# The last gate's products over eight steps of the last heads' attention in place of four, and two features' buffers taken in another order

## The chip, the cores and the metric

The kernel runs on one core of a Trainium2 chip. Its engines are TensorE (PE, with PEld for its weight loads), VectorE (DVE), ScalarE (ACT), GpSimd (POOL) and SyncE (SP), each with a queue of its own that it works off in order; data moves by DMA. The metric is the device time of one execution in microseconds (us), as the median of several runs.

## What is computed

A two-layer encoder over 1024 frames and 16 learned meta tokens (T = 1040), 1024 features. Half of a layer's features come from gated linear attention (GLA, 4 heads), half from softmax attention with a forget bias (FoX, 8 heads); both go through one output projection, and a convolutional feed-forward part follows.

```python
for i in range(DEPTH):
    xn = rms_norm(h, attn_norm[i])
    gq, gk, gv, gr, glr, fq, fk, fv, ff = jnp.split(xn @ w_in[i], cuts, axis=-1)
    ...
    o_gla = rms_norm(o_gla, gla_norm[i].reshape(GLA_HEADS, GLA_DV)).reshape(B, L, GLA_WIDTH)
    o_gla = o_gla * jax.nn.silu(gr)
    log_f = jax.nn.log_sigmoid((ff + b_forget[i]).astype(jnp.float32))
    o_fox = forgetting_attention(...)
    o_fox = rms_norm(o_fox, fox_norm[i].reshape(FOX_HEADS, FOX_DH)).reshape(B, L, FOX_WIDTH)
    h = h + jnp.concatenate([o_gla, o_fox], axis=-1) @ w_out[i]
    h = h + conv_ffn(rms_norm(h, ffn_norm[i]), w_up[i], conv_w[i], conv_b[i], w_down[i])
```

## The kernel before

Features lie on partitions, time along the free axis. Every product of two fp32 matrices is made of three matmuls over high and low parts (`mm3`, L253 to L255): high by high, low weight by high, high weight by low. Such a group is called a triple here. An operand is split by `split`: the high half on ACT (L378), the low half on DVE (L379); `xh`/`xl` are the halves of the normed input, `mh`/`ml` those of the attention's output ("mix", eight pairs: features 0 to 3 from GLA, 4 to 7 from FoX). Weights arrive as `raw` and are split by ACT L220 and DVE L222.

**The attention's steps.** `fox` runs 72 steps for a layer and eight more that only finish what is pending. There are four pairs of FoX heads (p = 0 to 3), 18 steps each: five groups of query tiles of 116 rows, two heads, the tiles of the group. Pair p = 3 begins at step 54, so its steps are 54 to 71. At a step PE makes the scores of one query tile (L706, L707, tile `S`); DVE adds the bias and takes the maximum (L714, two instructions for each piece); ACT takes the exponential (L722). Two steps later PE transposes the result (L743, tile `tr`), and ACT and DVE copy the transposes into `PT`, as high and low halves (L378, L379). Three steps behind the last tile of a head's group PE multiplies PT with V (L761, tile `av`), one step later follow the normalisation ("fold", L774 to L789), and two after that the transposed store. For p = 0 to 2 the store writes feature 4 + p to DRAM (`mixd`, L808); for p = 3 it writes feature 7 straight into its mix pair (L381, L382, and L800). GpSimd adds the causal mask to the bias ahead of a score (L879). PSUM holds five banks for `S` and `tr` together, two for `mm` and one for `av`.

**The fill.** Between these pieces PE gets other matmuls, from a list `work`. `plan(p)` makes the list anew when step `starts[p]` comes, after the old one has been drained; the list's rest is spread evenly over the steps that are left until the next start:

```python
starts = [f + 4 for f in first] + [first[3] + 8, len(steps) + 8]
...
fill_us = work.left / max(starts[p_next] - n, 1)
```

With `first` = 0, 18, 36, 54 the starts are 4, 22, 40, 58, 62 and 80. `plan(3)`, at step 58, is the gate of GLA head 3: `gr_products` multiplies the normed input with the gate's weights, three chunks of 348, 348 and 344 columns, the 344 last, eight features in each (24 triples), and each chunk is turned into feature 3 by six DVE operations (L666, L669, L673, L674, L675, L677) and three of ACT (L670 to L672), which write into the buffer `land[3]`. For the other heads the result goes to `mixd` (L679). Features 4, 5, 0, 1, 2 are loaded from `mixd` at the same time (L994).

`plan(4)`, at step 62, begins the output projection: it loads feature 6 (three pieces, L999), splits the seven features (`one`) chunk by chunk (columns 256, then 384, then 400), loads the residual `h` over each buffer once it is split (L1015, on POOL's queue), and multiplies for the first four of eight output tiles, three chunks each, seven features in the order `KORD` = 4, 5, 0, 1, 2, 3, 6; DVE adds the residual (L1020). Feature 7 and the other output tiles follow after the steps (tile `wo`).

**The buffers.** `slots` hands out 33 SBUF buffers of [128, T] from a list, first in, first out; a new user waits for the last readers of the old one. `land` are the seven buffers `h` of the unsplit features, `mix` the eight pairs. At `plan(4)` the pairs of the normed input (`nm["x"]`) and the norm's factor `r` go back to the list.

Names with numbers (`ml_6126`) are buffers in the tables of instructions below. They are not the same in the two kernels.

## Time and profile before

| | us |
|---|---|
| median of 3 runs | 2537.56 |
| lowest and highest run | 2532.59, 2539.26 |
| profiled execution, its own time | 2536.43 |
| its span in the trace | 2534.6 |
| granted TensorE clock over the span | 0.995 |

The span runs from the first to the last instruction of the profiled execution; the 1.8 us between span and time lie around it. Busy times are sums of an engine's instructions; a window's row gives them for one stretch, with the number of instructions in brackets. In a timeline's row, the first number is the start from the span's beginning, the second the length; matmuls overlap, so that the step from start to start is what one costs. A row's bracket gives the idle time of the engine ahead of it and what ended it. The changed stretch lies at about 437 to 505 us in layer 0 and 1690 to 1755 us in layer 1.

### The profile page before, as it was taken

The numbers are of one execution on the slowest core, as the hardware profiler recorded it, in microseconds if no ns is written. First come the engines' busy times: TensorE is split into PE (matmuls) and PEld (weight loads), VectorE is DVE, ScalarE is ACT, GpSimd is POOL, SyncE is SP. The second block draws the span as 40 slices with busy tenths as digits, with TensorE's granted clock in tenths as the row PEclk, the third lists the DMA queues.
The fourth block names the chain that finished last, engine by engine and source line by source line (L and its number), as shares of the span: only waits on it lengthen the run. The fifth ranks groups of instructions, "written<-read, shape, count | busy, mean of one in ns | idle before, by whom it ended". The sixth has DMA issues, their size and how long they took to land.

```text
span 2534.6 us, 48445 instructions
## 1 busy us (share of the span) xinstructions
PE 2475.4 (98%) x19266; PEld 2417.2 (95%) x19266; DVE 1741.0 (69%) x3373; ACT 1281.9 (51%) x2592; POOL 406.2 (16%) x582
## 2 busy tenths in 40 slices
PE   8999999999999999999999999999999999999998
PEld 7989999899999999999999899999999999999997
DVE  7656676859877777853565666677697777787545
ACT  7346666646444445641353566665464444455312
POOL 4033333210000000100211334331100000001002
PEclk9999999999999999999999999999999999999999
DMA  3132134342322224864312222143432222257622
GB/s 122 65 94 68 45 94 127 118 135 76 118 76 80 81 80 131 202 161 115 105 54 69 74 80 73 62 146 105 141 92 92 80 84 76 80 168 177 190 64 77
DMA packets 116211, 258.25 MB, mean 102 GB/s; under 512 B 14624, under 2 KB 31296, under 8 KB 115984
## 3 DMA queue, kind: packets, MB, share of 16 engines
q1 hardware_dynamic: 92832, 181.74, 23.0%
q0 software_dynamic: 22432, 72.68, 10.4%
q8 instruction: 151, 2.47, 0.4%
q10 hardware_dynamic: 720, 0.74, 0.1%
q14 instruction: 76, 0.62, 0.1%
HBM read 174.50 MB, written 67.81 MB: 96 GB/s over the span
## 4 chain that ended last, share of the span: by engine, by line
PE 83%; DVE 8%; ACT 3%; DMA 2%; issue 2%; POOL 1%; SPq 0%; DVEq 0%; POOLq 0%; ACTq 0%
PE up L253 11%; PE up L254 11%; PE up L255 11%; PE mm L253 8%; PE mm L255 7%; PE mm L254 7%; PE down L253 5%; PE down L254 5%; PE down L255 5%; PE av L761 3%; PE tr L743 2%; PE wo L253 1%; PE wo L255 1%; PE wo L254 1%; DVE P L714 1%
## 5 line engine op out<-in xcount | busy, mean ns | idle before, releaser
L253 PE MATMUL up<-x,hi 128*128 128x260 f32 (+1 forms) x2464 | 697.2, 283 | 2.2 <-DVE hg L1287 1.4
L255 PE MATMUL up<-x,hi 128*128 128x260 f32 (+1 forms) x2464 | 695.9, 282 | 2.4 <-DVE x L1109 2.4
L254 PE MATMUL up<-x,lo 128*128 128x260 f32 (+1 forms) x2464 | 696.6, 283 | 0.0
L255 PEld LDWEIGHTS up<-x,hi 128*128 128x128 f32 x2464 | 465.7, 189 | 3.2 <-DVE x L1109 3.2
L253 PEld LDWEIGHTS up<-x,hi 128*128 128x128 f32 x2464 | 464.5, 189 | 3.1 <-DVE hg L1287 1.8
L254 PEld LDWEIGHTS up<-x,lo 128*128 128x128 f32 x2464 | 464.6, 189 | 0.1
L1085 DVE TENSOR_TENSOR lo<-raw,hi 128x512 fp32r<-128x512 f32 x364 | 249.0, 689 | 178.2 <-ACT hi L1084 170.4
L253 PE MATMUL mm<-xh,hi 128*128 128x348 f32 (+4 forms) x1056 | 363.5, 344 | 0.0
L254 PE MATMUL mm<-xh,lo 128*128 128x348 f32 (+4 forms) x1056 | 339.7, 322 | 0.0
L255 PE MATMUL mm<-xl,hi 128*128 128x348 f32 (+4 forms) x1056 | 339.6, 322 | 0.0
L1084 ACT CAST hi<-raw 128x512 fp32r<-128x512 f32 x364 | 224.6, 621 | 144.2 <-PE up L255 84.8
L253 PEld LDWEIGHTS mm<-xh,hi 128*128 128x128 f32 x1056 | 200.2, 190 | 5.8 <-issue 4.6
L254 PEld LDWEIGHTS mm<-xh,lo 128*128 128x128 f32 x1056 | 200.0, 189 | 0.6 <-issue 0.3
L255 PEld LDWEIGHTS mm<-xl,hi 128*128 128x128 f32 x1056 | 198.9, 188 | 0.6 <-issue 0.3
L254 PE MATMUL down<-ah,lo 128*128 128x260 f32 (+1 forms) x704 | 198.3, 282 | 0.2 <-DVE lo L222 0.2
L255 PE MATMUL down<-al,hi 128*128 128x260 f32 (+1 forms) x704 | 198.2, 282 | 0.0
L253 PE MATMUL down<-ah,hi 128*128 128x260 f32 (+1 forms) x704 | 198.0, 281 | 0.0
L379 DVE TENSOR_TENSOR PT<-tr,PT 116x464 fp32r<-116x464 f32 (+3 forms) x240 | 122.7, 517 | 71.9 <-ACT PT L378 69.7
L220 ACT CAST hi<-raw 128x512 fp32r<-128x512 f32 (+1 forms) x160 | 97.1, 609 | 148.0 <-PE down L255 116.5
L743 PE MATMUL tr<-ident,P 116*116 116x116 f32 x704 | 144.8, 269 | 3.0 <-DVE m L714 2.5
L722 ACT ACTIVATE P<-P,m 116x924 f32<-116x924 f32 (+4 forms) x144 | 110.6, 768 | 70.8 <-DVE m L714 65.2
L1312 POOL DMA_DIRECT2D actd<-cv x44 | 23.6, 537 | 766.1 <-DVE cv L1311 745.1
(300 smaller groups left out, 5782.0 us busy)
## 6 DMA issues: line engine op xcount, KB each, us to landing
raw<-in_wm_dram SPq DMA_DIRECT2D x322, 256.0 KB, 2.8
raw<-in_wd_dram SPq DMA_DIRECT2D x64, 256.0 KB, 3.7
actd<-cv POOLq DMA_DIRECT2D x22, 520.0 KB, 3.0
actd<-cv POOLq DMA_DIRECT2D x22, 512.0 KB, 3.1
cb<-cd SPq DMA_DIRECT2D x16, 520.0 KB, 4.3
st<-actd SPq DMA_DIRECT2D x14, 520.0 KB, 5.4
st<-actd SPq DMA_DIRECT2D x14, 512.0 KB, 5.7
kA<-kA SPq DMA_DIRECT2D x24, 260.0 KB, 4.3
```

Source lines behind the costliest of these rows:

```text
L220: nc.scalar.copy(hi[:, :n, :], raw[:, :n, :])
L253: nc.tensor.matmul(ps, wh, xh[:, c0:c0 + n], start=first, stop=False, skip_group_check=more)
L254: nc.tensor.matmul(ps, wl, xh[:, c0:c0 + n], start=False, stop=False, skip_group_check=more)
L255: nc.tensor.matmul(ps, wh, xl[:, c0:c0 + n], start=False, stop=last, skip_group_check=more)
L379: nc.vector.tensor_tensor(out=lo, in0=src, in1=hi.bitcast(F32), op=ALU.subtract)
L714: nc.vector.tensor_tensor_reduce(out=x, in0=S[:rows, :n], in1=cb[:rows, c0:k1], scale=1.0, scalar=(BIG if ci == 0 else m[:rows, ci - 1:ci] ...
L722: nc.scalar.activation(x, x, AF.Exp, scale=-1.0, bias=low, accum_out=(den if nch < 3 else d2[:rows, 0:1]))
L743: nc.tensor.transpose(tr[:w, j, :rows], P[:rows, o:o + w], id_)
L761: nc.tensor.matmul(av[:, a:width], w.rearrange("p a b -> p (a b)"), x, start=(t == 0 and i == 0), stop=(t == last and i == 1))
L1084: nc.scalar.copy(hi[:, :nk, :], src[:, :nk, :])
L1085: nc.vector.tensor_tensor(out=lo[:, :nk, :], in0=src[:, :nk, :], in1=hi[:, :nk, :].bitcast(F32), op=ALU.subtract)
L1312: nc.gpsimd.dma_start(self.actd[j][:, o0:T], uo)
```

## The change

The start of `plan(4)` moves from step 62 to step 66, so that the gate's 72 matmuls of `plan(3)` spread over steps 58 to 65. What `plan(4)` issues moves with it. `plan(3)` now takes six `h` buffers and the eighth mix pair (`seven`), which the last store needs ahead of step 66. `plan(4)` first gives back the normed input's buffers, then takes the buffer of feature 6, loads into it, and takes seven mix pairs.

```diff
-        starts = [f + 4 for f in first] + [first[3] + 8, len(steps) + 8]
+        starts = [f + 4 for f in first] + [first[3] + 12, len(steps) + 8]
...
                     elif p == 3:
-                        land = box["land"] = [s.get(F32, f"h{k}") for k in range(KD - 1)]
+                        land = box["land"] = [s.get(F32, f"h{k}") for k in range(KD - 2)]
+                        box["seven"] = s.get(F32R, "mh7"), s.get(F32R, "ml7")
                         for k in (4, 5, 0, 1, 2):
                             nc.gpsimd.dma_start(land[k][:, :T], self.mixd[k][:])
                         self.gr_products(lyr, 3, w, ap, pp, nm, land[3])
                     elif p == 4:
-                        land = box["land"]
-                        for c0, n in reversed(CH):
-                            nc.gpsimd.dma_start(land[6][:, c0:c0 + n], self.mixd[6][:, c0:c0 + n])
                         for x in nm["x"]:
                             s.put(*x)
                         s.put(nm["r"])
-                        mix = box["mix"] = [(s.get(F32R, f"mh{k}"), s.get(F32R, f"ml{k}")) for k in range(KD)]
+                        land = box["land"] + [s.get(F32, "h6")]
+                        for c0, n in reversed(CH):
+                            nc.gpsimd.dma_start(land[6][:, c0:c0 + n], self.mixd[6][:, c0:c0 + n])
+                        mix = [(s.get(F32R, f"mh{k}"), s.get(F32R, f"ml{k}")) for k in range(KD - 1)] + [box["seven"]]
+                        box["mix"] = mix
...
-                self.fox(lyr, ap, pp, qs, plan, lambda: box["mix"][KD - 1])
+                self.fox(lyr, ap, pp, qs, plan, lambda: box["seven"])
```

On PE the projection's first triple before stands right behind the scores of step 62 (460 and 116 columns, the transposes of step 60 between them):

```order
L706 MATMUL S<-kA_4642,qA_4640 116x460
L707 MATMUL S<-kL_4644,qA_4640 116x460
L743 MATMUL tr<-ident,P 116x116
L706 MATMUL S<-kA_4642,qA_4640 116x116
L743 MATMUL tr<-ident,P 116x116
L707 MATMUL S<-kL_4644,qA_4640 116x116
L743 MATMUL tr<-ident,P 116x116
L253 MATMUL mm<-mh_6121,hi 128x256
L254 MATMUL mm<-mh_6121,lo 128x256
L255 MATMUL mm<-ml_6122,hi 128x256
```

In the changed kernel it stands behind the scores of step 66 (344 columns), and the last gate triples (`xh`, `xl`) come ahead of them, behind step 65:

```order
L253 MATMUL mm<-xh_147,hi 128x344
L254 MATMUL mm<-xh_147,lo 128x344
L255 MATMUL mm<-xl_148,hi 128x344
L774 MATMUL fo<-ident,avs 116x128 x4
L761 MATMUL av<-PT_6158,V_4646 128x232 x8
L743 MATMUL tr<-ident,P 116x116
L706 MATMUL S<-kA_4642,qA_4640 116x344
L707 MATMUL S<-kL_4644,qA_4640 116x344
L743 MATMUL tr<-ident,P 116x116 x3
L253 MATMUL mm<-mh_6272,hi 128x256
L254 MATMUL mm<-mh_6272,lo 128x256
L255 MATMUL mm<-ml_6273,hi 128x256
```

The gate's products have moved by up to four steps, and the projection's by four. On DVE the low halves before stand in steps 60 to 63; this is the place of step 62, from its score on (`h_5795` is feature 6, `h_5792` feature 3, which L677 finishes here):

```order
L714 ISA P,m<-S,cb 116x460
L714 ISA m 116x1
L677 SCALAR_TENSOR_TENSOR h_5792<-gy,gog 128x344
L714 ISA P,m<-S,cb,m 116x116
L714 ISA m 116x1
L379 TENSOR_TENSOR PT_6152<-tr,PT_6152 116x4x116
L379 TENSOR_TENSOR ml_6126<-h_5795,mh_6125 128x256
L379 TENSOR_TENSOR ml_6122<-h_5793,mh_6121 128x384
L379 TENSOR_TENSOR ml_6124<-h_5794,mh_6123 128x384
L379 TENSOR_TENSOR ml_6116<-h_5790,mh_6115 128x384
L379 TENSOR_TENSOR ml_6118<-h_5791,mh_6117 128x384
```

In the changed kernel the low halves begin in step 63. This is DVE from the score of step 65 on, where the last gate chunk (L666 to L673) and the fold (L778) stand among them; `h_6260` is feature 6:

```order
L714 ISA P,m<-S,cb 116x460
L714 ISA m 116x1
L379 TENSOR_TENSOR ml_6273<-h_5793,mh_6272 128x256
L379 TENSOR_TENSOR PT_6158<-tr,PT_6158 116x4x116
L666 TENSOR_TENSOR gx<-mm,r 128x344
L379 TENSOR_TENSOR ml_6275<-h_5794,mh_6274 128x256
L669 TENSOR_SCALAR ge<-gx 128x344
L673 TENSOR_TENSOR gog<-gx,gog 128x344
L778 TENSOR_TENSOR ff<-fo,ff 116x256
L222 TENSOR_TENSOR lo<-raw,hi 128x512
L379 TENSOR_TENSOR ml_6277<-h_6260,mh_6276 128x256
```

The last low half that the projection's first chunk needs (feature 6) has moved from the score of step 62 to that of step 65 on DVE, while its product has moved from step 62 to step 66 on PE. The low halves' number, and that of every other instruction on PE, DVE and ACT, is the same in both.

## The prediction

> **What bounds the kernel now.** I read the page's head and busy line first, then TensorE's waits, then the stretch around the edit in tables by window and in time order.

> ```profile
> span 2534.6 us, 48445 instructions
> PE 2475.4 (98%) x19266; PEld 2417.2 (95%) x19266; DVE 1741.0 (69%) x3373; ACT 1281.9 (51%) x2592; POOL 406.2 (16%) x582
> ```

> TensorE (PE) is busy for 98% of the span, so nothing can be gained except where PE waits or runs at a lower clock. The edit adds and removes no instruction on PE, DVE or ACT, so its worth lies in those waits. The next rows are a wait table (total, times, longest), first for the whole trace, then for the stretch 418 to 480 us of layer 0, and PE's timeline at the three long waits (start, length, instruction, in brackets the idle time before it).

> ```profile
> PE mm L255 <- DVE ml L379: 7.2, 4, 3.0
> ...
> PE S L706 <- DVE m L714: 0.8, 1, 0.8
> ...
> PE tr L743 <- DVE m L714: 0.3, 1, 0.3
> PE S L706 <- DVE PT L379: 0.2, 1, 0.2
> ```

> ```profile
> 466.19 0.39 PE L255 MATMUL mm<-ml,hi 128*128 128x256 f32 x1 [0.65 <-DVE ml L379]
> ...
> 470.19 0.50 PE L255 MATMUL mm<-ml,hi 128*128 128x256 f32 x1 [2.97 <-DVE ml L379]
> ...
> 1720.98 0.58 PE L255 MATMUL mm<-ml,hi 128*128 128x256 f32 x1 [2.96 <-DVE ml L379]
> ```

> The reader is to see one place per layer: the output projection's first chunk waits 0.65 and then 2.97 us for the low half of features that DVE splits; both layers together lose 7.2 us. The tables by window (length, then busy time of PE, PEld, DVE, ACT, POOL, the granted clock, DMA) say why and what follows.

> ```profile
> 457.00:480.00 23.00, 19.37 (x130) 18.26 (x129) 22.88 (x66) 16.98 (x44) 8.38 (x16) 0.93 0.46 139
> 470.20:473.70 3.50, 3.50 (x13) 3.26 (x14) 3.50 (x9) 2.48 (x8) 1.38 (x3) 0.51 0.16 33
> 1720.90:1726.50 5.60, 5.52 (x20) 5.19 (x21) 5.25 (x14) 3.74 (x11) 2.08 (x4) 0.51 0.27 72
> ```

> From 457 to 480 us DVE is busy for 22.88 of 23.00 us: there **DVE is the bound**, and PE waits for it. Right after the wait the granted clock is 0.51 for 3.5 us in layer 0 and for 5.6 us in layer 1, which costs 3.5 x 0.49 = 1.7 and 5.6 x 0.49 = 2.7 us. Three smaller waits at step 59 of layer 0 (0.8, 0.3, 0.2, by their rows in time 0.77, 0.25, 0.21) add 1.2; layer 1 has none there. All that the edit could save is so 7.2 + 1.7 + 2.7 + 1.2 = **12.8 us**, 0.5% of the span.

> **The change part by part.** Durations are taken from start to start in rows that follow one another without a wait.

> ```profile
> 459.68 0.32 PE L253 MATMUL mm<-xh,hi 128*128 128x344 f32 x1
> ...
> 460.15 0.32 PE L253 MATMUL mm<-xh,hi 128*128 128x344 f32 x1
> ...
> 461.81 0.44 PE L706 MATMUL S<-kA,qA 128*116 128x460 f32 x1
> ...
> 462.68 0.36 PE L253 MATMUL mm<-mh,hi 128*128 128x256 f32 x1
> ...
> 466.41 0.28 PE L253 MATMUL mm<-mh,hi 128*128 128x256 f32 x1
> 466.53 0.28 PE L254 MATMUL mm<-mh,lo 128*128 128x256 f32 x1
> ...
> 474.62 0.33 PE L255 MATMUL mm<-ml,hi 128*128 128x384 f32 x1
> ...
> 475.15 0.34 PE L255 MATMUL mm<-ml,hi 128*128 128x384 f32 x1
> 475.32 1.05 PE L761 MATMUL av<-PT,V 112*128 112x232 f32 x8
> 476.21 0.26 PE L743 MATMUL tr<-ident,P 116*116 116x116 f32 x1
> ```

> So a gate triple takes 0.47 us, a matmul of the projection 0.12 (256 columns) or 0.53 / 3 = 0.18 (384), a step's scores with their transposes 0.87, a block of eight av products 0.89.

> ```profile
> 458.37 0.63 DVE L714 CUSTOM_DVE_ANT_0 P<-S,cb 116x460 f32<-116x460 f32 x1
> 458.92 0.08 DVE L714 DVE_READ_ACCUMULATOR2_ANT m<- 116x1 f32 x1
> ...
> 460.20 0.64 DVE L379 TENSOR_TENSOR PT<-tr,PT 116x464 fp32r<-116x464 f32 x1
> 460.75 0.52 DVE L675 SCALAR_TENSOR_TENSOR gy<-ge,gy 128x348 f32<-128x348 f32 x1
> 461.19 0.42 DVE L379 TENSOR_TENSOR ml<-h,mh 128x256 fp32r<-128x256 f32 x1
> 461.53 0.51 DVE L677 SCALAR_TENSOR_TENSOR h<-gy,gog 128x348 f32<-128x348 f32 x1
> ...
> 464.43 1.29 DVE L222 TENSOR_TENSOR lo<-raw,hi 128x512 fp32r<-128x512 f32 x2
> ...
> 469.71 2.29 DVE L379 TENSOR_TENSOR ml<-h,mh 128x256 fp32r<-128x256 f32 x5
> ...
> 475.44 3.48 DVE L379 TENSOR_TENSOR ml<-h,mh 128x400 fp32r<-128x400 f32 x7
> 478.83 0.63 DVE L714 CUSTOM_DVE_ANT_0 P<-S,cb 116x460 f32<-116x460 f32 x1
> ```

> On DVE a score takes 0.55 + 0.09, a copy of four transposes (PT) 0.55, a low half 0.34 at 256 columns, 3.39 / 7 = 0.48 at 400 and about (2.21 - 0.34) / 4 = 0.47 at 384, a gate operation 0.43 (the clamp of L669 0.25, taken from its neighbours), a weight split 0.6.

> *The start of the projection, from step 62 to 66.* The 72 gate matmuls (24 triples, 11.3 us) are spread over eight steps, and the projection's products begin four steps later. With order and durations, PE's steps 63 to 67 now hold 27 gate matmuls (4.3), 21 + 21 of the projection (2.5 + 3.7), 6 steps' score products (2.0), 31 transposes (2.8) and 32 av products (3.6): **18.9 us**. DVE's same steps hold all 21 low halves (7 x 0.33 + 7 x 0.47 + 7 x 0.48 = 8.9), two gate chunks (2 x 2.4), nine PT copies (3.4), six scores (3.1), two weight splits (1.2), the last head's halves and fold (2.0) and two residual adds (0.8): **24.2 us**. The long wait goes, but the DVE work that caused it is not moved with PE's: some 7 us of PE's filler leave steps 58 to 68 for the steps after the last head, where DVE is idle, and in steps 63 to 67 DVE is short of time by 24.2 - 18.9 = 5.3 us. What is late next is not the projection's operand but the attention itself.

> I follow it from PE's score of step 63 (t = 0), DVE's loads from score to score being 5.5, 4.7, 5.3, 4.5 and 4.2 us. DVE takes up score 63 at 0.75 and, with some 0.75 of small waits on ACT as an estimate, score 64 at 7.0. PE's steps 63 and 64 take 3.7 + 3.2 with small gaps, so that it wants a bank for score 65 at 6.9; it gets one when DVE has copied the transposes of step 64, behind score, low half, small score and copy: 7.0 + 0.64 + 0.34 + 0.28 + 0.55 = 8.8. **PE waits 2.0.** DVE's score 65 comes at 7.0 + 4.7 = 11.7 and the next PT copy is done at 11.7 + 0.64 + 0.34 + 0.55 = 13.2; PE's score, transposes, nine gate matmuls and fold have then taken 2.6 since 8.9, so the av products wait 13.2 - 11.5 = **1.7**. The scores 66, 67 and 68 come to DVE at 17.0, 21.5 and 25.7; PE reaches the av products of step 68 at 22.4 and their PT is done 1.9 behind score 67, at 23.4: **1.0**. Sum 4.7 us per layer, of the 5.3 that the loads gave; the buffers hold the rest.

> *Step 59.* With the fill of steps 58 to 61 halved, PE comes to the score of step 59 three triples earlier, 1.41 us. DVE is held there by the store of an earlier gate chunk, which the edit does not touch.

> ```profile
> 441.68 0.34 DVE L669 TENSOR_SCALAR ge<-gx 128x348 f32<-128x348 f32 x1 [1.91 <-DMA mixd<-ge]
> ...
> 1692.53 0.34 DVE L669 TENSOR_SCALAR ge<-gx 128x348 f32<-128x348 f32 x1 [0.25 <-DMA mixd<-ge]
> ```

> One gate operation (0.44) moves behind DVE's second score of step 58, so layer 0 waits 1.2 + 1.4 - 0.4 = **2.2 us**; in layer 1, whose hold is 0.25 and whose slack I estimate at 0.3, 1.4 - 0.4 - 0.3 = **0.7**.

> *The buffers.* Feature 6 is now loaded into the buffer of xh0, behind PE's last reading of it, which stands ahead of the score of step 64, while its first product follows step 66: more than 7 us for loads that land in 2.7 (from issue to landing, 200 KB).

> ```profile
> h<-mixd POOLq DMA_DIRECT2D x2, 200.0 KB, 2.7
> ```

> They stand on POOL's queue behind the mask of step 64 and ahead of the residual loads and of the mask for step 65, whose score DVE takes at 11.7; with xh0 read by about 3 they have over 8 us. I cost them at nothing; without that cover each microsecond is one of PE's wait. The last pair's buffers are taken before the store that fills them, at nothing.

> *Sum.* After: 2 x 4.7 + 2.2 + 0.7 = 12.3, and the clock stays up if no wait reaches the 2.97 that preceded the fall. Before: 12.8. The difference is -0.5 us, on the profiled execution's 2536.43 gives 2535.9, which lies 1.7 below the median of the runs (2537.56). **I forecast 2536.0 us.** The unshown price is what a wait of about 2 us does to the clock: nothing, or in each layer a window like those above. The bounds are so 0 and 2 x 2.7 = 5.4 us; I take 0, by the nearest row (the wait of 0.65 at 466.19 is followed by products of 0.12 us, full speed).

> [...]

> **The rivals.** *First, the waits of after are hidden.* DVE's shortage needs the order and rates as I have them; if banks come free earlier (ACT shares the PT copies, four steps' lead) and PE is never held in steps 63 to 68, after has no more than step 59's 2.9 us at worst and about 0.4 at best. The gain is 12.8 - 2.9 to 12.8 - 0.4, say 11: 2525.5 us. For it speaks that DVE starts step 63 with little behind it (a load of 1.9 us in step 62 against PE's 3.4); against it the sum of loads, 5.3 us that five banks cannot hold.

> *Second, on the other side: the clock falls all the same.* The waits of 2.0 and 1.7 lie within some 6 us, and PE's halved filler leaves no reserve. If together they bring the clock to 0.51 for as long as in layer 1 (5.6 us), each layer loses 2.7 more; some of it is absorbed, as PE would have waited 1.0 behind. That is +3.4 to +5.4: 2539.3 to 2541.3. If at the same time DVE's lag is 7 rather than 4.7 per layer, 4.6 more: about 2546, slower than the bound below. It decides from the point where the two waits together pass the 3.6 us of before: mine give 3.7 in two pieces.

> *Third, the change does not do what it says:* the long wait stays, as feature 6 comes late in the new buffer. Then 12.8 stays and step 59's 1.7 is added: 2538. The over 7 us of cover speak against it.

> **How the numbers follow.** About 0.3% (7.6 us) is what a measurement of this kernel can tell from no change. Chances: my sum, with an error of some 4 us either way, 0.62; the first rival 0.16; the second 0.16, half of it beyond 0.3%; the third 0.06. Faster by over 0.3%, below 2530: the first rival with 0.02 of the sum's lower edge, 0.18. Slower, above 2545: 0.08. The rest is 0.74. The range goes from 2528.5 to 2543.5: it leaves out most of the first rival and the worst of the second.

> **What would show it.** In the wait table of after, the 7.2 us on the projection's low halves are gone, and in their place stand waits of PE's score and av products for DVE's PT and scores, 4 to 5 us per layer, none over 2.5; step 59's wait in layer 0 is about 2 us; the clock between steps 63 and 68 stays near 1.0; and DVE's busy share there is near 100%. I am wrong if PE shows under 3 us of waits per layer there (first rival), or a window at half clock (second).

## The result, and the profile after

The changed kernel takes 2549.05 us (median of 5 runs, 2544.11 to 2551.03), the kernel before 2534.35 in the same comparison (5 runs, 2532.12 to 2539.26). The ratio is **1.0044, with a 95% interval from 1.0033 to 1.0056**: slower by some 11 us, 8 to 14 by the interval (the two medians alone lie 14.7 us apart). The forecast was 2536.0. The profiled execution took 2549.36 us.

First the page's head and busy line of the changed kernel:

```profile
span 2547.6 us, 48454 instructions
PE 2480.7 (97%) x19266; PEld 2420.5 (95%) x19266; DVE 1742.6 (68%) x3373; ACT 1281.4 (50%) x2592; POOL 407.0 (16%) x582
```

PE, PEld, DVE, ACT and POOL have as many instructions as before (the head's total is 9 higher; the busy line does not show them), and nearly the same busy times: what was added is waiting. These are TensorE's waits in the stretch of layer 0 (420 to 533 us; total, times, longest):

```profile
PE av L761 <- DVE PT L379: 3.1, 4, 1.2
PE tr L743 <- DVE m L714: 2.0, 1, 2.0
PE S L706 <- DVE m L714: 1.5, 2, 1.0
PE av L761 <- ACT PT L378: 1.2, 1, 1.2
...
PE fo L774 <- ACT avs L764: 0.5, 1, 0.5
```

The wait for the projection's low halves (7.2 us in both layers) is gone. In its place layer 0 has 8.3 us of waits of the attention's own matmuls, layer 1 7.8 by the same view; before, the same stretches had 5.5 and 3.9 us, the projection's included. (A wait of 0.8 us at the first `wo` matmul, which both kernels have in both layers, is left out of these sums.) In time order, TensorE's waits of layer 0 (bracket: idle time and what ended it):

```profile
429.27 0.32 PE L761 MATMUL av<-PT,V 112*128 112x112 f32 x1 [1.24 <-DVE PT L379]
...
446.12 0.31 PE L743 MATMUL tr<-ident,P 116*116 116x116 f32 x1 [2.02 <-DVE m L714]
446.85 0.47 PE L706 MATMUL S<-kA,qA 128*116 128x460 f32 x1 [0.42 <-DVE m L714]
...
468.50 1.05 PE L761 MATMUL av<-PT,V 112*128 112x232 f32 x7 [1.15 <-DVE PT L379]
...
473.84 0.47 PE L706 MATMUL S<-kA,qA 128*116 128x460 f32 x1 [1.05 <-DVE m L714]
...
476.82 0.54 PE L774 MATMUL fo<-ident,avs 128*116 128x128 f32 x3 [0.47 <-ACT avs L764]
...
478.56 0.38 PE L761 MATMUL av<-PT,V 112*128 112x232 f32 x1 [1.20 <-ACT PT L378]
479.29 1.84 PE L761 MATMUL av<-PT,V 112*128 112x232 f32 x7 [0.36 <-DVE PT L379]
```

The rows lie at step 55 (429), step 59 (446), the end of step 63 (468), the scores of step 65 (473.84) and the end of step 65 (476 to 479). The tables by window (length, busy time of PE, PEld, DVE, ACT, POOL, granted clock, DMA) show steps 65 to 67 of both layers, and three windows in which the clock fell:

```profile
473.84:492.04 18.20, 16.17 (x95) 15.20 (x95) 18.17 (x52) 13.42 (x38) 7.18 (x13) 0.81 0.55 168
1731.55:1748.36 16.81, 14.79 (x94) 13.86 (x95) 16.81 (x49) 13.42 (x38) 6.10 (x11) 0.90 0.54 165
...
448.20:451.40 3.20, 3.20 (x14) 2.99 (x13) 2.98 (x9) 1.66 (x5) 0.55 (x1) 0.50 0.33 111
478.90:485.70 6.80, 6.44 (x31) 6.34 (x30) 6.80 (x19) 6.80 (x21) 1.08 (x2) 0.50 0.59 218
1738.30:1741.70 3.40, 3.40 (x19) 3.40 (x17) 3.40 (x11) 3.40 (x10) 0.23 (x1) 0.51 0.76 282
```

DVE is busy for 18.17 of 18.20 and 16.81 of 16.81 us in steps 65 to 67, and the clock is at half for 13.4 us in all, against 9.1 us before (waits at its start left out); taken at half of that, the loss is 6.7 us against 4.4. This is an estimate, and a little high: in the changed kernel a matmul of 256 columns took 0.21 us from start to start at half clock and 0.12 elsewhere (medians of 23 and 1984).

The account: waits in the two stretches went from 9.4 to 16.1 us (+6.7), the clock costs 2.3 more, together +9.0. From the first score of step 54 to the first `wo` matmul TensorE took 106.40 us in layer 0 and 105.26 in layer 1 before, and 112.31 and 109.22 after: **+5.9 and +4.0, so +9.9 us**. The 0.9 left stands in no wait and in no half-clock window. Over the runs below, what is left in this way grows with the number of waits, by some 0.27 us for each (an estimate, from a straight line through both layers of the 17 traces with the same matmuls; e4 against e5 has 21 waits against 9, and 3.0 us are left); by this estimate a wait costs a little more than its length. The two profiled executions differ by 12.9; the other 3.0 lie in small parts in other stretches and were not followed.

The table gives the time from one step's first score to the next one's, from those rows of each trace (layer 0 / layer 1, us); e4, e5, e9 and e13 are experiments below.

| steps | before | after | e5 (62, store moved) | e4 (66, store moved) | e9 (e4, no low halves) | e13 (e9, late high halves) |
|---|---|---|---|---|---|---|
| 58 | 7.1 / 5.7 | 7.1 / 6.1 | 5.7 / 5.7 | 4.8 / 4.6 | 4.8 / 4.5 | 4.8 / 4.5 |
| 59 to 61 | 17.0 / 16.7 | 14.2 / 14.2 | 16.9 / 16.9 | 14.3 / 14.0 | 14.0 / 14.5 | 14.0 / 14.2 |
| 62, 63 | 14.4 / 15.4 | 8.4 / 8.4 | 14.4 / 15.1 | 8.2 / 8.4 | 8.4 / 8.2 | 8.4 / 8.4 |
| 64 | 3.9 / 3.8 | 4.4 / 4.4 | 3.9 / 3.8 | 4.4 / 4.4 | 4.0 / 4.0 | 3.7 / 3.7 |
| 65 to 67 | 12.3 / 12.2 | 18.2 / 16.8 | 12.3 / 12.2 | 16.9 / 16.4 | 18.6 / 18.4 | 14.3 / 14.3 |
| 54 to `wo` | 106.4 / 105.3 | 112.3 / 109.2 | 104.9 / 105.2 | 108.2 / 106.5 | 108.7 / 108.7 | 104.6 / 104.0 |

The long stall of steps 62 and 63 is gone, and steps 65 to 67 take 4 to 6 us more. The filler that left comes back behind them: steps 68 to 70 take 2.0 us more in either layer, the last step and its tail up to the `wo` matmul 5.3.

### The profile page after: what moved, and what is told of

The parts are those of the page before. It is cut to its first block, busy times and chain, and to the rows that moved or that the text cites. A ratio compares the mean times of both kernels' runs of the same rounds, so it can differ in the third digit from the quotient of the medians.

```text
span 2547.6 us, 48454 instructions
## 1 busy us (share of the span) xinstructions
PE 2480.7 (97%) x19266; PEld 2420.5 (95%) x19266; DVE 1742.6 (68%) x3373; ACT 1281.4 (50%) x2592; POOL 407.0 (16%) x582
## 4 chain that ended last, share of the span: by engine, by line
PE 50%; issue 31%; DVE 11%; DMA 4%; ACT 3%; POOL 2%; SPq 0%; DVEq 0%; POOLq 0%; ACTq 0%
PE mm L253 8%; PE mm L255 7%; PE mm L254 7%; PE down L253 5%; PE down L255 5%; PE down L254 5%; PE av L761 3%; PE tr L743 2%; DVE P L714 1%; PE wo L253 1%; PE wo L255 1%; PE wo L254 1%; DVE lo L1087 1%; DMA mixd<-ge 1%; PE S L706 1%
## 5 line engine op out<-in xcount | busy, mean ns | idle before, releaser
L253 PE MATMUL up<-x,hi 128*128 128x260 f32 (+1 forms) x2464 | 697.1, 283 | 2.4 <-DVE hg L1289 1.4
L255 PE MATMUL up<-x,hi 128*128 128x260 f32 (+1 forms) x2464 | 696.4, 283 | 2.3 <-DVE x L1111 2.3
L254 PE MATMUL up<-x,lo 128*128 128x260 f32 (+1 forms) x2464 | 696.7, 283 | 0.0
L255 PEld LDWEIGHTS up<-x,hi 128*128 128x128 f32 x2464 | 465.2, 189 | 3.1 <-DVE x L1111 3.1
L253 PEld LDWEIGHTS up<-x,hi 128*128 128x128 f32 x2464 | 464.5, 188 | 3.5 <-DVE hg L1289 1.8
L254 PEld LDWEIGHTS up<-x,lo 128*128 128x128 f32 x2464 | 464.8, 189 | 0.1
L253 PE MATMUL mm<-xh,hi 128*128 128x348 f32 (+4 forms) x1056 | 366.1, 347 | 0.0
L255 PE MATMUL mm<-xl,hi 128*128 128x348 f32 (+4 forms) x1056 | 341.4, 323 | 0.0
L254 PE MATMUL mm<-xh,lo 128*128 128x348 f32 (+4 forms) x1056 | 341.1, 323 | 0.0
L253 PEld LDWEIGHTS mm<-xh,hi 128*128 128x128 f32 x1056 | 201.2, 191 | 5.9 <-issue 4.6
L254 PEld LDWEIGHTS mm<-xh,lo 128*128 128x128 f32 x1056 | 201.2, 191 | 0.6 <-issue 0.3
L255 PEld LDWEIGHTS mm<-xl,hi 128*128 128x128 f32 x1056 | 200.3, 190 | 0.6 <-issue 0.3
L254 PE MATMUL down<-ah,lo 128*128 128x260 f32 (+1 forms) x704 | 198.2, 282 | 1.4 <-DVE lo L222 1.4
L255 PE MATMUL down<-al,hi 128*128 128x260 f32 (+1 forms) x704 | 198.5, 282 | 0.0
L253 PE MATMUL down<-ah,hi 128*128 128x260 f32 (+1 forms) x704 | 198.2, 281 | 0.0
L379 DVE TENSOR_TENSOR PT<-tr,PT 116x464 fp32r<-116x464 f32 (+3 forms) x240 | 122.5, 516 | 70.8 <-ACT PT L378 68.5
L743 PE MATMUL tr<-ident,P 116*116 116x116 f32 x704 | 144.6, 269 | 5.8 <-DVE m L714 5.3
L1069 DVE TENSOR_TENSOR raw<-raw,raw 128x512 f32<-128x512 f32 x198 | 129.8, 688 | 25.3 <-DMA raw<-in_wd_dram 19.1
```

Of the source, the lines that this page charges most:

```text
L253: nc.tensor.matmul(ps, wh, xh[:, c0:c0 + n], start=first, stop=False, skip_group_check=more)
L254: nc.tensor.matmul(ps, wl, xh[:, c0:c0 + n], start=False, stop=False, skip_group_check=more)
L255: nc.tensor.matmul(ps, wh, xl[:, c0:c0 + n], start=False, stop=last, skip_group_check=more)
L379: nc.vector.tensor_tensor(out=lo, in0=src, in1=hi.bitcast(F32), op=ALU.subtract)
L743: nc.tensor.transpose(tr[:w, j, :rows], P[:rows, o:o + w], id_)
L1069: nc.vector.tensor_tensor(out=q[out][:, :nk, :], in0=q[a][:, :nk, :], in1=q[b][:, :nk, :], op=op)
```

## The experiments

Each was compared with the kernel before on the same chip; ratios are to it, with the 95% interval. One thousandth is 2.5 us.

**e1: the order of buffers alone.**

```diff
-        starts = [f + 4 for f in first] + [first[3] + 12, len(steps) + 8]
+        starts = [f + 4 for f in first] + [first[3] + 8, len(steps) + 8]
```

> The start of the projection back at step 62, the changed order of buffers kept. Theory A (VectorE's low halves and gate work hold up the attention in steps 62 to 67, and TensorE's waits there and at step 59 bring the clock down, all because the filler moved): the time is near that of before, 2532 to 2540 us, with the long wait for a low half back. Rival B (feature 6 in the buffer of xh0 comes late and delays the rest): 2545 us or more, with waits of ScalarE for the load of feature 6.

Measured: 2540.18 us, 1.0014 [1.0005, 1.0022]. The buffers alone cost some 3.5 us, 1.3 to 5.6. No wait for the load of feature 6 shows on TensorE or on ScalarE; TensorE's waits for low halves are 2.8 and 3.3 us per layer, and waits for PT of 1.2 us stand beside them. Rival B, 10 us, falls; but the buffers are not free, as both the forecast and theory A had it.

**e2: the start half way**, `first[3] + 10`.

> The projection starts at step 64, half way. Theory A: between the two, 2535 to 2545 us, the waits for PT and scores smaller than the 4.5 us per layer of the changed kernel in these steps, the wait for low halves under 1 us. Rival (only the clock windows matter, not the waits): the time jumps to either end, by whether a window at half clock is there.

Measured: 2543.15 us, 1.0035 [1.0022, 1.0048], in the range of theory A. Rival "only the clock windows matter", which had the time jump to either end, falls. But the waits did not shrink as expected: for low halves none is left, and for PT and scores steps 62 to 67 have 5.2 us in layer 0 and 4.8 in layer 1, where less than 4.5 was forecast.

**e3: the later low halves kept back on VectorE.** `self.scored` is the latest score instruction on VectorE; `issue_after` puts what is written in it behind that instruction on the same engine.

```diff
                             def one(k):
-                                self.split(mix[k][0][:, c0:c0 + n], mix[k][1][:, c0:c0 + n], land[k][:, c0:c0 + n])
+                                if j == 2:
+                                    self.split(mix[k][0][:, c0:c0 + n], mix[k][1][:, c0:c0 + n], land[k][:, c0:c0 + n])
+                                    return
+                                with tc.issue_after(self.scored.ins):
+                                    self.split(mix[k][0][:, c0:c0 + n], mix[k][1][:, c0:c0 + n], land[k][:, c0:c0 + n])
```

> The changed kernel with the low halves of the second and third chunk (384 and 400 columns) kept behind the score of the step in which their unit is written, so that VectorE makes them later, behind the attention's work. Theory A: the waits of steps 62 to 67 fall from 4.5 to under 2 us per layer and the half-clock windows behind them (6.8 us long in layer 0, 3.4 in layer 1) go; 8 to 11 us less than the changed kernel, about 2538 to 2541 us. Rival C (the gate's evacuation or ScalarE holds the attention, not the low halves): no more than 3 us less, 2546 to 2549 us.

Measured: 2549.65 us, 1.0057 [1.0046, 1.0069]: nothing gained. A window of its trace shows where the wait went:

```profile
469.00:477.00 8.00, 5.61 (x30) 4.73 (x28) 6.32 (x16) 8.00 (x24) 2.16 (x4) 0.77 0.43 150
```

DVE is now busy for 6.32 of 8.00 us, but ACT for all of them. The edit held back the low halves only; ACT went on making high halves early, and TensorE waited for ACT's `avs` and `PT`. Of the two forecasts rival C, no gain, was met; theory A as I had it, VectorE alone, fell here.

**e4: the store taken from another tile.** In the kernels shown, the gate's result of heads 0 to 2 stands in the tile `ge`, of which there is one, until it is stored; the next chunk waits for that.

```diff
-            to = e if dst is None else dst[:, c0:c0 + n]
+            to = og if dst is None else dst[:, c0:c0 + n]
...
-                nc.gpsimd.dma_start(self.mixd[h][:, c0:c0 + n], e)
+                nc.gpsimd.dma_start(self.mixd[h][:, c0:c0 + n], og)
```

> The changed kernel, with the gate's result for heads 0 to 2 written into and stored from the tile of the output gate (two buffers) in place of the exponent's tile (one buffer), so that the next gate chunk no longer waits for the store. Theory A: the waits at step 59 (2.0 + 0.4 us and a half-clock window of 3.4 us in layer 0, 1.1 + 0.4 in layer 1) go: about 5 us less, 2544 us. Rival (TensorE comes to step 59 early and waits for VectorE in any case): no change, 2549 us.

Measured: 2537.11 us, 1.0008 [0.9999, 1.0016], some 9 us less than the changed kernel by the ratios; I had expected 5. Step 58 falls from 7.1 and 6.1 to 4.8 and 4.6 us. VectorE's row in the changed kernel's timeline shows the hold that went, 2.58 us against 1.91 before:

```profile
444.78 0.34 DVE L669 TENSOR_SCALAR ge<-gx 128x348 f32<-128x348 f32 x1 [2.58 <-DMA mixd<-ge]
```

The same trace holds the best view of the clock. These are TensorE's waits at the end of step 65 in layer 0 and in layer 1, and the windows behind them:

```profile
470.18 0.54 PE L774 MATMUL fo<-ident,avs 128*116 128x128 f32 x3 [0.47 <-ACT avs L764]
471.92 0.37 PE L761 MATMUL av<-PT,V 112*128 112x232 f32 x1 [1.20 <-ACT PT L378]
472.65 1.38 PE L761 MATMUL av<-PT,V 112*128 112x232 f32 x7 [0.36 <-DVE PT L379]
...
1724.28 0.54 PE L774 MATMUL fo<-ident,avs 128*116 128x128 f32 x3 [0.48 <-ACT avs L764]
1726.02 0.37 PE L761 MATMUL av<-PT,V 112*128 112x232 f32 x1 [1.20 <-ACT PT L378]
1726.75 1.05 PE L761 MATMUL av<-PT,V 112*128 112x232 f32 x7 [0.36 <-DVE PT L379]
```

```profile
473.20:476.70 3.50, 3.50 (x19) 3.43 (x18) 3.50 (x11) 3.50 (x11) 0.00 (x0) 0.51 0.78 290
1727.20:1730.70 3.50, 3.50 (x33) 3.48 (x32) 3.50 (x11) 3.50 (x10) 0.00 (x0) 1.00 0.82 286
```

Behind the same three waits, 2.0 us within 3, the clock was 0.51 in layer 0 and 1.00 in layer 1.

**e5: the same edit on the kernel before.**

> The kernel before, with only the store of the gate's result taken from the tile of the output gate (as in e4). It is the base against which e4 is read. If the store's hold costs only what shows at step 59 of layer 0: 1 to 2 us less than before, 2533 to 2535 us. If e4's gain of 12 us came from everywhere: 2526 us or less, and the start at step 66 would then still cost some 11 us over this.

Measured: 2529.77 us, 0.9981 [0.9972, 0.9990]: 5 us faster than before, more than I had put down to step 59, and faster than both kernels. Against this base e4 is slower by 2.7 thousandths, 7 us: **that is what the later start costs without the store's hold, buffers included** (some 4 to 10 us by the two intervals; the last row of the table shows 4.5 of it). In that stretch TensorE's waits are 4.1 us longer in e4 and the rest, which grows with their number, 3.0, while the clock costs 2.5 less (1.7 against 4.2): without the hold it is not the clock that makes the later start slower.

**e6: e4 with the later halves kept back on both engines**, behind `self.exped[-2]`, the exponential of the step before the last, on ScalarE; the low halves need the high ones and follow.

> e4 (start at step 66, store from the output gate's tile), with the high halves on ScalarE of the second and third chunk, and so the low halves that follow them, kept behind the exponentials of the step before the last. Theory D (halves made too early on both engines stand ahead of the copies that the attention waits for): the waits for PT and avs in steps 62 to 66, 5 to 6 us per layer in e4, fall to under 3, and no half-clock window follows: 2530 to 2533 us. Rival E (the chain from score to PT is too long for steps of 3.4 to 5 us, whatever else the engines do): no change, 2536 to 2539 us.

Measured: 2537.05 us, 1.0007 [0.9998, 1.0016], as e4. No window at half clock is left, yet steps 65 to 67 of layer 0 are no shorter:

```profile
466.13:483.61 17.48, 14.37 (x94) 12.06 (x95) 16.69 (x48) 14.99 (x43) 5.67 (x11) 1.00 0.39 125
```

DVE is busy for 16.69 of 17.48 us, and waits for low halves (1.6 us) and PT (3.5) stand where those for ACT stood. By the time rival E was met and theory D was not; but with VectorE this full, the load and the order could not yet be told apart.

**e7: e4 with more matmuls in steps 63 to 65.** The 24 matmuls of the last gate chunk are issued twice (`if twice: self.mm3(...)` ahead of the real one), so that the gate's argument is doubled in these 344 columns.

> e4, with each triple of the last gate chunk (steps 63 to 65) multiplied twice into the same sum, so that this gate is that of a doubled argument in 344 columns: 24 more matmuls of 0.16 us per layer, 7.5 us of TensorE time in all, with nothing added on the other engines. If TensorE only waits in these steps for the others (theory D and rival E alike), the matmuls fill waits and keep the clock up: 2534 to 2540 us. If the waits are not what costs the time there: 2544 us or more.

Measured: 2539.72 us, 1.0019 [1.0011, 1.0028], 2.8 us above e4 for 7.5 us of work, in the range for "fills waits": some 4.7 of it, by the difference and with its noise of some 3 us, stood in time that TensorE would have lost anyway.

**e8: e5 with a gate product on GpSimd**, `nc.gpsimd.tensor_tensor` in place of `nc.vector.tensor_tensor` for L673.

> e5, with the product of the gate's argument and the output gate (L673) on GpSimd in place of VectorE, in all gate chunks. Of the kernel before, theory A says that VectorE is the bound at steps 60 to 62 and that the 3 us wait shrinks by what is taken off it, three operations of 0.43 us: about 1.3 us per layer, and the half-clock window may go with it: 2528 to 2532 us. Rival: GpSimd takes longer and the gate is later: 2535 us or more.

Measured: 2545.73 us, 1.0041 [1.0027, 1.0055], 15 us slower than e5; the rival held. The operation took 984 ns there on average (24 of them), by the groups of its trace:

```profile
L673 POOL TENSOR_TENSOR gog<-gx,gog 128x348 f32<-128x348 f32 (+1 forms) x24 | 23.6, 984 | 21.6 <-DVE gx L666 20.4 <-DVE fv L785 1.2
```

The wait for low halves fell to 2.1 us per layer, as hoped, but waits for scores and PT came in its place all over the attention.

**e9 and e10: the low halves left out.** TensorE multiplies the high half in their place; the seven features' low parts are missing from the projection. e9 has the start at step 66, e10 at step 62.

```diff
-                                self.split(mix[k][0][:, c0:c0 + n], mix[k][1][:, c0:c0 + n], land[k][:, c0:c0 + n])
+                                nc.scalar.copy(mix[k][0][:, c0:c0 + n], land[k][:, c0:c0 + n])
```

> e4 (start at step 66), with the low halves of the seven features left out: TensorE multiplies the high half once more in their place, as many matmuls as before, and VectorE has 21 operations (8.9 us) less per layer in these steps. Theory A (VectorE is the bound in steps 65 to 67, where it was busy for 100% of 16.4 to 18.2 us): TensorE's waits in steps 62 to 67 fall from 5 to 6 us to about 2 per layer, steps 65 to 67 from 16.9 and 16.4 us to 13 to 14: 2529 to 2532 us. Rival E (the latency of the chain from score to PT, or ScalarE): steps 65 to 67 stay above 15.5 us, 2535 us or more.

> e5 (start at step 62) without the same low halves. Theory A: the 3 us wait at step 62 and its half-clock window go, 5 to 6 us per layer: 2518 to 2521 us, and e9 stands above it by what the chain's latency alone costs at the later start. If VectorE is the only reason against the later start, e9 and e10 agree within 3 us; if the thinner filler costs by itself (rival E), e9 is 6 us or more above e10.

Measured: e9 2537.64 us, 1.0005 [0.9994, 1.0017]; e10 2531.99 us, 0.9988 [0.9978, 0.9998]. Both forecasts were missed: with 8.9 us of VectorE's work per layer gone, neither is faster than with it beyond the intervals (e4 1.0008, e5 0.9981). Rows of e9, layer 0: steps 65 to 67 by window, two of TensorE's waits, and ScalarE's queue at that time.

```profile
466.70:485.26 18.56, 16.17 (x95) 15.11 (x95) 11.74 (x34) 14.00 (x40) 5.16 (x11) 0.82 0.69 234
```

```profile
470.29 0.54 PE L774 MATMUL fo<-ident,avs 128*116 128x128 f32 x3 [1.09 <-ACT avs L764]
472.02 2.52 PE L761 MATMUL av<-PT,V 112*128 112x232 f32 x8 [1.19 <-ACT PT L378]
```

```profile
468.45 1.53 ACT L1014 CAST mh<-h 128x256 fp32r<-128x256 f32 x4
469.89 0.34 ACT L764 COPY avs<-av 128x232 f32<-128x232 f32 x1
470.13 0.25 ACT L378 CAST PT<-tr 116x116 fp32r<-116x116 f32 x1
470.28 1.25 ACT L1014 CAST mh<-h 128x256 fp32r<-128x256 f32 x3
471.43 0.54 ACT L378 CAST PT<-tr 116x464 fp32r<-116x464 f32 x1
```

DVE is now free for 7 of 18.6 us, and still nothing is gained (at a clock of 0.82, 3.3 of the 18.6 us are the half clock's): the copies that TensorE waits for stand on ScalarE behind four and behind three high halves.

**e11: e5 with the start at step 63.**

> e5 with the start at step 63, one step later, buffers as before. Theory A: one step more for the 256-column low halves makes the long wait shorter, but the filler per step falls by a fifth and VectorE's work in the steps behind stays: within 4 us of e5, 2528 to 2534 us. If only the long wait matters: 2526 us or less.

Measured: 2530.58 us, 0.9979 [0.9968, 0.9990], as e5. The waits for low halves fall to 1.4 us per layer, those for PT rise to 2.0 and 3.0.

**e12: e1 with e4's store.**

> e1 (start at step 62, buffers in the new order) with the store from the output gate's tile. If the 3.5 us that e1 lost come from step 58 and the store's hold: 2529 to 2531 us, as e5. If they come from steps 61 and 62 (feature 6 or another order on VectorE): 2532 to 2534 us.

Measured: 2532.56 us, 0.9988 [0.9977, 0.9998], 1.8 us above e5 by the ratios; the intervals overlap, so that little more than the direction can be said.

**e13 and e14: both queues relieved**, e9 and e10 with the later high halves kept back as in e6.

> e9 (start at step 66, no low halves) with the high halves of the second and third chunk on ScalarE kept behind the exponentials of the step before the last, as in e6. VectorE has 8.9 us less per layer and ScalarE its early halves later. Theory F (two queues: with the low halves VectorE holds the attention, with early high halves ScalarE does, and taking away one leaves the other): the waits of steps 64 to 67, 3.5 to 4 us per layer in e9, fall to about 1, no half-clock window: 2529 to 2532 us. Rival E (the chain from score to PT is too long for the thinner filler): 2535 us or more.

> e10 (start at step 62, no low halves) with the high halves kept back in the same way. Theory F: the wait for ScalarE's PT at step 63 (1.8 us) and the half-clock window behind it go: 2522 to 2526 us. Rival E: as e10, 2530 us or more.

Measured: e13 2531.13 us, 0.9983 [0.9974, 0.9992], 2.2 thousandths below e9; e14 2526.34 us, 0.9964 [0.9953, 0.9976], 2.4 below e10. Steps 65 to 67 of e13's layer 0:

```profile
468.26:482.53 14.27, 13.34 (x94) 12.43 (x95) 11.18 (x33) 13.49 (x39) 5.07 (x10) 1.00 0.47 148
```

They fall from 18.56 to 14.27 us; 3.3 of these 4.3 us are the clock, which stays at full speed now. **Theory F is shown** by four runs with the start at step 66: with both loads 1.0008 (e4), with the order relieved alone 1.0007 (e6), with the low halves gone alone 1.0005 (e9), with both 0.9983 (e13), whose interval is clear of the other three. VectorE's low halves and ScalarE's high halves each hold the attention up, and taking away one leaves the other. But e13 still stands 1.9 thousandths, 5 us, above e14. Rival E, a chain that the thinner filler doesn't cover, would explain that; no run tests it by itself.

**e15 and e16: nothing left out**, e5 and e11 with the later halves kept back on both engines as in e6.

> e5 (start at step 62, store from the output gate's tile) with all halves in place and those of the second and third chunk kept back on both engines, as in e6. A version meant to be used. Theory F: fewer halves stand ahead of the seven that the first chunk needs, so the 3 us wait at step 62 shortens; VectorE's sum of work stays, so some of it comes back behind: 2525 to 2529 us against 2530 of e5. Rival: the 256-column halves themselves are late, no change, 2529 to 2531 us.

> The same with the start at step 63 (e11). Theory F: as e15, within 3 us of it, 2525 to 2530 us.

Measured: e15 2530.95 us, 0.9984 [0.9974, 0.9994]; e16 2533.11 us, 0.9997 [0.9988, 1.0006]. No better than e5, and e16 rather worse (its interval only just overlaps that of e5). With the low halves in place the order alone gains nothing, and without them it does (e14 against e10): that points to VectorE's load. e5, and e11 as well as it, beat both kernels, e5 by 1.9 thousandths against before.

## Why the prediction was wrong

The direction was missed, and the time lies above the range and above 2546, the worst that I had put down. The account of the profile splits the miss: the sum said -0.5, the traces say +9.0 for waits and clock. The clock makes 6.7 us of the difference, waits at places for which the sum had no term 2.8. By the steps of the prediction:

- **What bounds, and the 12.8 us at stake**: right as far as it went. But I took 7.2 + 4.4 + 1.2 us for all that the edit could move, and it could also add.
- **What is late next** ("not the projection's operand but the attention itself"): right. The long wait went, and waits of `S`, `av` and `fo` came. Steps 63 to 67 were forecast to wait 4.7 us per layer; the rows of layer 0 from 468.50 to 479.29 give 1.15 + 1.05 + 0.47 + 1.20 + 0.36 = 4.2 us, and layer 1 has the same. The single places were partly others: the score of step 65 was there (2.0 forecast, 1.05 measured), the wait of step 68 was not.
- **The engine named**: half right. DVE is at 100% in steps 65 to 67, and its load in steps 63 to 67 is what the sum said (24.2 us forecast, 25.9 and 24.5 in the two layers). I left ScalarE out of the sum, though it makes a high half for every low half in the same steps; e9 shows that it holds the attention just as long once VectorE doesn't.
- **Step 59**: in layer 0 the forecast for the waits held, 2.2 us against 2.02 + 0.42; in layer 1 0.7 were forecast and 1.5 came. With steps 63 to 67 the two terms add up to the 12.3 us that the sum had, in part by luck, as 1.0 too little here meets 1.0 too much there. Step 59's price did not hold: a half-clock window of 3.2 us came behind it in layer 0. Without the store's hold the changed kernel is some 9 us faster (e4), but not all of that hung on step 59: the edit frees the store of every chunk of heads 0 to 2, and the kernel before gains 5 us by it too (e5). What the later start makes of the hold is the difference, about 4.
- **The clock**, "I take 0, by the nearest row": **this is the step that failed.** I measured each wait by itself against the 2.97 us that came ahead of the fall before. Ahead of the falls came 2.02 + 0.42 in layer 0, and 0.47 + 1.20 there (the 0.36 came when the clock was already down); in layer 1 all three, 2.0 us together. The price is 6.7 us, above my upper end of 5.4, where I had counted 4.4 saved and none spent. It turns the sum by itself: -0.5 + 6.7 = +6.2. The second rival was this mechanism, with a chance of 0.16 and its condition (the two waits pass 3.6 us together) set too high. The trace of before had a nearer row, outside the stretch that I looked at: ahead of the changed steps of layer 1, a window at 0.50 came behind two waits of 2.0 us together.

```profile
1612.21 0.31 PE L743 MATMUL tr<-ident,P 116*116 116x116 f32 x1 [0.76 <-DVE m L714]
1613.79 0.73 PE L706 MATMUL S<-kA,qA 128*116 128x460 f32 x1 [1.26 <-DVE m L714]
```

```profile
1613.90:1617.10 3.20, 3.20 (x12) 2.90 (x13) 2.87 (x8) 2.32 (x6) 1.12 (x2) 0.50 0.28 87
```

- **The buffers**, "at nothing": e1 puts them at 3.5 us (1.3 to 5.6) at the early start. Which of their waits they cause was not settled: the load of feature 6 shows in none of the waits of TensorE and ScalarE, and with e4's store the cost is 1.8 us, within the noise (e12 against e5).
- **Not foreseen**: waits at places without a term in the sum, 3.8 us in both layers against 1.0 before. The largest is 1.24 us at step 55 (0.8 in layer 1), ahead of the place where the change begins; before, the same place waited 0.3 in layer 0 and e4 has 0.78 there. Layer 1 has 0.44 and 0.52 more behind the scores of step 59. Why step 55 waits longer stays open.

What the runs show in place of the sum: the later start costs 7 us by itself (e4 against e5). The reading that fits the four runs behind theory F is that the work of VectorE and ScalarE, which had steps of some 5.6 us of TensorE at its side (59 to 61), now has 4.2 to 4.7 (59 to 64). It costs more where a hold of one engine meets a TensorE that comes earlier, as at step 59, and where a window at half clock comes behind the short waits that follow (0.50 behind 2.02 + 0.42 us).

## What to carry to other kernels

A filler on the busiest engine also gives the others time: before moving it away from a stretch, add up every engine's work there, not only that of the one that waits today. If two queues carry halves of the same job, relieving one may show nothing (1.0007 in e6 and 1.0005 in e9, against 1.0008 in e4); relieve both before a theory is dropped (0.9983 in e13). And short waits are to be added up over a few us when the clock is priced, not taken one by one: in e4 three of 1.20 us and less stood ahead of a clock of 0.51.

## What the runs showed of the hardware

A granted clock of a half came behind waits much shorter than the 2.97 us of before: behind 2.0 us in three pieces, the longest 1.20, in e4's layer 0, and the same three pieces left it at 1.00 in its layer 1. In the changed kernel's two stretches no wait was longer than 2.02 us, and the clock fell three times.

```profile
469.77:473.18 3.41, 1.45 (x8) 1.02 (x9) 3.41 (x10) 3.41 (x11) 2.26 (x5) 1.00 0.84 212
1722.46:1725.87 3.41, 1.88 (x12) 1.34 (x11) 3.41 (x10) 3.41 (x12) 2.22 (x5) 1.00 0.64 182
1725.87:1729.28 3.41, 2.90 (x22) 2.70 (x23) 3.41 (x9) 3.41 (x11) 0.88 (x2) 1.00 0.95 295
```

TensorE is idle for 1.96 us in the first, and for 1.53 and 0.51 in the other two. That layer 1 kept its clock because its waits were shared in this way is my reading, and was not shown.

GpSimd took 935 ns (median of 24, 922 to 1377, e8) for a product of 128x348 (128x344 in 8 of them) that took VectorE 510 (504 to 601, e5); moving the 24 of them cost 15 us (e8 against e5).
